# The opening of a two-layer diffusion backbone: modulation weights in column pieces, sums of squares on TensorE

## The chip, the cores and the metric

The kernel runs on one NeuronCore of a Trainium2 chip. The core has TensorE (matrix products, written PE in the trace, its weight loads PEld), VectorE (DVE), ScalarE (ACT), GpSimd (POOL) and SyncE (SP, which here only issues DMAs). Each engine works through its own list of instructions in order. The metric is the device time of one execution in microseconds; lower is better.

## The reference, cut to what matters

Two layers run over 256 latent and 256 context tokens of width 1024. Every sub-layer begins with a norm whose scale and shift come from a conditioning vector, one vector for latent tokens and one for context tokens (two "classes"). The change concerns only the first sub-layer of layer 0:

```python
m_lat = split(silu(c) @ w_ada[l] + b_ada[l], 9)       # shift, scale, gate of three sub-layers
m_ctx = split(silu(c_ctx) @ w_ada[l] + b_ada[l], 9)
y = x * rsqrt(mean(x * x, -1) + EPS)                  # rmsnorm, then * norm_g
h = y * norm_g * (1 + scale) + shift                  # modulate
a, b = split(h @ ffn_w1, 2)                           # D = 1024 -> 2 * 2816
x = x + 0.5 * gate * ((silu(a) * b) @ ffn_w2)
```

Shift and scale of this first norm are the first 2 x 1024 columns of `w_ada[0]`. All nine vectors of the other norms are computed later, beside dense products, by another routine.

## The kernel before, in words

Activations lie transposed: channels on the 128 partitions in 8 chunks (`kc`), 512 tokens along the free side, context in columns 0 to 255, latents in 256 to 511. A dense product is done as three products in a rounded 32-bit format (`three`, lines 230 to 234): weights and activations are each split into a high part (`hi`, a cast on ScalarE, line 219) and a low part (`lo`, a subtraction on VectorE, line 220), and hi x lo, hi x hi and lo x hi are added up in PSUM. The first of the three uses the low part of the activations, so a chunk's products start only when the low parts of both classes are there.

A unit of `ffn_w1` is 128 output columns: 128 x 1024 numbers in one DMA of 512 KB into a ring of four `raw` buffers. Two units, a and b, give one tile of the hidden layer. TensorE's order is the order of the program; the other engines' lists are ordered by a scheduler at build time, by priorities, so an instruction can stand ahead of one that was written earlier.

The opening of the program is `cold_start` (line 413). What stands around the change:

- SyncE issues, in order: the conditioning vector, `x` in 8 DMAs of 256 KB, four DMAs of the first half of the scale's columns (512 columns; `room`, line 164), two units of `ffn_w1`, four DMAs of the first half of the shift's columns, four more units, then the second halves of scale and shift (eight DMAs).
- The sum of squares of each token is a chain over the 8 chunks and two classes: a square on ScalarE (line 257), an addition on VectorE (line 258). Four transpositions on TensorE, a reduction on VectorE, a scaling and a power of -1/2 on GpSimd (lines 263 to 271) give 1/rms per token, and two pairs of transpositions spread it over partitions (line 281; ScalarE copies it to `junk`, line 428).
- Scale and shift are products of `sc` (silu of the two conditioning vectors, padded to 32 columns) with `w_ada` (line 169): four column groups of TensorE at once, each one block of 128 columns, all 8 chunks accumulated. ScalarE copies the result (`rows`, line 174), one transposition brings channels onto partitions (line 177), VectorE adds the bias (line 182) and forms norm_g * (1 + scale) (line 184).
- `norm_part` (line 286) makes one chunk and class of the activations: `u` on VectorE (line 289), the high part on ScalarE (line 291), the low part on VectorE (line 292).
- Six units (`FIRST`) are worked in two parts. Part 0 runs chunks 0 to 3 of units 0-1, 2-3, 4-5; part 1 runs chunks 4 to 7 of units 4-5, 0-1, 2-3. The products for the second halves of scale and shift are fed between the dense products of part 0 and the start of part 1, at the counts listed in `COLD`. After that the program goes on with the other 38 units of `ffn_w1`, one pair at a time.

Of the kernel before, what the change touches and what calls it, by code (L numbers as in the profile page):

```python
# [16 lines left out]
P = 128  # L17
# [33 lines left out]
EARLY = 2  # L51
COLD = ((4, 6, 8, 10, 12, 13), (10, 12, 14, 16, 17, 18))
# [59 lines left out]
def tile_backbone(ctx: ExitStack, tc: tile.TileContext, I, out: bass.AP):  # L112
# [45 lines left out]
    def ada_first(l, mod, part, room):  # L158

        pa = psum()  # L160
        c0 = mod * D + part * 512
        for k2 in range(KC // 2):
            raw = room[:, k2, :]
            nc.sync.dma_start(out=raw.rearrange("p (k c) -> p k c", k=2),
                              in_=I["w_ada0"][k2 * 256:(k2 + 1) * 256, c0:c0 + 512].rearrange("(k p) c -> p k c", k=2))
            for k in range(2):
                kc = 2 * k2 + k
                for j in range(4):
                    mm(pa[32 * j:32 * j + 32, 0:P], sc[:, kc, :], raw[:, k * 512 + j * P:k * 512 + (j + 1) * P],
                       start=kc == 0, stop=kc == KC - 1)  # L170
            yield
        rows = np_.tile([P, 256], F32, tag="rows", name="rows", bufs=1)[:, 0:P]
# [5 lines left out]
        ks = slice(4 * part, 4 * part + 4)  # L178
        v = pt[:, 0:P].rearrange("p (j c) -> p j c", j=4)
        with tc.high_priority(offset=AHEAD):  # L180
            for cls in range(2):
                nc.vector.tensor_tensor(modT[l][:, mod, cls, ks], v[:, :, cls], b_ada[:, l, mod, ks], ALU.add)
                if mod % 3 == 1:
                    nc.vector.scalar_tensor_tensor(amod[l][:, mod // 3, cls, ks], modT[l][:, mod, cls, ks], 1.0,
                                                   norm_g[:, l, mod // 3, ks], ALU.add, ALU.mult)
# [36 lines left out]
    def weights(src, n=1024, extra=None, soon=False, room=None, behind=None):  # L222
        raw = wp.tile([P, 1024], F32, tag="raw", name="raw", bufs=4)
        nc.sync.dma_start(out=raw[:, :n], in_=src)
        hi, lo = room or ((extra or wp).tile([P, 1024], F32R, tag=tag, name=tag) for tag in ("whi", "wlo"))
        with tc.high_priority(offset=AHEAD if soon else WSOON):
            split(hi[:, :n], lo[:, :n], raw[:, :n], behind)
        return hi, lo
# [57 lines left out]
    def norm_part(l, which, h, kc, cls, rb):  # L286
        cs = SLICES[cls]
        u = np_.tile([P, 256], F32, tag="u", name="u", bufs=UB)
        nc.vector.scalar_tensor_tensor(u, x[:, kc, cs], amod[l][:, which, cls, kc:kc + 1], rb, ALU.mult, ALU.mult)
        shift = modT[l][:, 3 * which, cls, kc:kc + 1]  # L290
        lead[cls, kc] = nc.scalar.activation(h[0][:, kc, cs], u, AF.Identity, bias=shift).ins
        nc.vector.scalar_tensor_tensor(h[1][:, kc, cs], u, shift, h[0][:, kc, cs].bitcast(F32),  # L292
                                       ALU.add, ALU.subtract)
# [67 lines left out]
    def ada_all(vectors, pool, junk):  # L361
        if not vectors:
            return
        scb = pool.tile([P, 2, 512], F32, name="scb")
# [12 lines left out]
    def ffn(l, i, classes, out_classes_next, before, vectors):  # L377
# [35 lines left out]
        def cold_start(n):  # L413

            rooms = glo.before(F32, [P, KC, 1024])
            scale, shift = ([ada_first(l, 3 * which + what, part, rooms[:, 4 * (1 - what):4 * (1 - what) + 4, :])
                             for part in (0, 1)] for what in (1, 0))
            for dt in range(KC):
                for at in SLICES:
                    square_sum(dt, at)  # L420
            rows = [rstd_rows(at) for at in SLICES]
            next(scale[0])
            for r in rows:
                next(r)
            rb = junk.rearrange("p (a t) -> p a t", a=2)
            for cls, r in enumerate(rows):
                next(scale[0])
                nc.scalar.copy(rb[:, cls], next(r)[:, 0:256])
            ws = []

            def load(ks):
                for k in ks:
                    ws.append(w1_unit(k, room=kept(k) if k < 4 else None, soon=k < 2))

            for _ in scale[0]:
                pass
            load(range(EARLY))
            for _ in shift[0]:
                pass
            load(range(EARLY, n))  # L440
            pts = [psum() for _ in range(n)]
            beside.at(scale[1], COLD[0])
            beside.at(shift[1], COLD[1])
            for part, order in enumerate(((0, 2, 4), (4, 0, 2))):
                if part:
                    beside.drain()
                with tc.high_priority(offset=AHEAD):
                    for kc in range(4 * part, 4 * part + 4):
                        for cls in (0, 1):
                            norm_part(l, which, h, kc, cls, rb[:, cls])  # L450
                for k in order:
                    for kc in range(4 * part, 4 * part + 4):
# [4 lines left out]
                    if part:  # L457
                        act(k // 2, pts[k], pts[k + 1])
# [926 lines left out]
```

## Time and profile before

| | |
|---|---|
| time, median of 3 runs | 2267.32 us (2265.69 to 2268.48) |
| the profiled execution's own time | 2266.51 us |
| its span, first to last instruction | 2264.7 us |
| first dense product starts | 26.89 us |
| first product behind the six opening units | 67.63 us |
| TensorE busy over the span | 2234.9 us, 99% |

The span is what the trace's rows add up to; 1.8 us of the profiled execution lie outside it. TensorE is nearly always busy, so the time is its list of products plus the stretches in which it waits or runs at the lower of its two clocks, 1.2 in place of 2.4 GHz ("granted clock" 0.50 in the rows). A product's duration in the trace includes its latency; how fast products follow each other is read from the difference of their starts.

### The profile page before, as it was taken

Reading aid. Unit: us, or ns where it says so; the run is one execution under the profiler, and the core shown is the slowest. Engines: PE = TensorE matmul, PEld = TensorE weight load, DVE = VectorE, ACT = ScalarE, POOL = GpSimd, SP = SyncE. Lnnn points to the kernel's source line nnn. Section 1 sums busy time; section 2 is a strip of 40 time slices with the busy share of each in tenths; the row PEclk is TensorE's granted clock in tenths of the full one; section 3 lists DMA queues with packets and bytes.
Section 4 is the critical chain, followed back from the end, with each engine's and each line's share of the span. In section 5 each row is a group of like instructions: output and inputs, shape, how many; then the busy total and the mean of one; then the engine's idle time right before and its main releaser. Section 6 shows DMA issues by size and latency. Waiting matters only on the chain.

```text
span 2264.7 us, 33530 instructions
## 1 busy us (share of the span) xinstructions
PE 2234.9 (99%) x12799; PEld 1935.7 (85%) x12799; DVE 1579.1 (70%) x3388; ACT 934.4 (41%) x1675; POOL 81.3 (4%) x137
## 2 busy tenths in 40 slices
PE   7999999999999999999999999999999999999998
PEld 4888889888888888888888898888898898899998
DVE  5989843887665664676666579998258885768664
ACT  4323222455654553333222232322234675656443
POOL 0000000001001110000000000000000001200000
PEclk9999999999999999999999999999999999999999
DMA  8556542322223332344544436666333244445564
GB/s 305 184 198 204 192 139 89 112 66 75 75 76 93 91 87 84 99 144 140 159 147 149 141 113 208 208 200 195 101 99 112 67 140 121 135 155 169 188 184 131
DMA packets 94033, 315.53 MB, mean 139 GB/s; under 512 B 12928, under 2 KB 13712, under 8 KB 93872
## 3 DMA queue, kind: packets, MB, share of 16 engines
q1 hardware_dynamic: 89072, 308.07, 42.3%
q0 software_dynamic: 2144, 4.36, 1.4%
q8 instruction: 100, 1.64, 0.3%
q10 hardware_dynamic: 2656, 0.96, 0.2%
q14 instruction: 61, 0.50, 0.1%
HBM read 312.30 MB, written 1.05 MB: 138 GB/s over the span
## 4 chain that ended last, share of the span: by engine, by line
PE 86%; issue 9%; DVE 3%; DMA 1%; ACT 1%; SPq 0%; POOLq 0%; POOL 0%; DVEq 0%; ACTq 0%
PE p L232 25%; PE p L233 24%; PE p L234 24%; PE p L649 2%; PE p L650 2%; PE p L651 2%; PE p L674 1%; PE p L916 1%; PE p L1131 1%; PE p L971 1%; PE p L970 1%; PE p L1041 1%; DMA room<-in_w_ada 1%; PE p L893 1%; DVE wlo L220 1%
## 5 line engine op out<-in xcount | busy, mean ns | idle before, releaser
L219 ACT CAST whi<-raw 128x1024 fp32r<-128x1024 f32 (+1 forms) x430 | 444.7, 1035 | 823.7 <-PE p L233 715.7
L220 DVE TENSOR_TENSOR wlo<-raw,whi 128x1024 fp32r<-128x1024 f32 (+1 forms) x430 | 516.6, 1202 | 268.5 <-ACT whi L219 266.8
L232 PE MATMUL p<-h,whi 128*128 128x512 f32 (+1 forms) x1856 | 695.5, 375 | 0.2 <-DVE h L292 0.2
L234 PE MATMUL p<-h,wlo 128*128 128x512 f32 (+1 forms) x1856 | 681.1, 367 | 0.0
L233 PE MATMUL p<-h,whi 128*128 128x512 f32 (+1 forms) x1856 | 681.1, 367 | 0.0
L232 PEld LDWEIGHTS p<-h,whi 128*128 128x128 f32 x1856 | 348.7, 188 | 58.7 <-issue 2.4
L234 PEld LDWEIGHTS p<-h,wlo 128*128 128x128 f32 x1856 | 348.6, 188 | 58.4
L233 PEld LDWEIGHTS p<-h,whi 128*128 128x128 f32 x1856 | 349.1, 188 | 56.5 <-issue 1.9
L233 PE MATMUL p<-ghi,whi 128*128 128x256 f32 (+1 forms) x836 | 278.0, 333 | 0.0
L234 PE MATMUL p<-ghi,wlo 128*128 128x256 f32 (+1 forms) x836 | 277.8, 332 | 0.0
L197 DVE SCALAR_TENSOR_TENSOR junk<-raw,scb 128x512 f32<-128x512 f32 x256 | 176.2, 688 | 112.7 <-DMA raw<-in_w_adaT 112.2
L232 PE MATMUL p<-glo,whi 128*128 128x256 f32 (+1 forms) x616 | 201.9, 328 | 0.0
L197 DVE SCALAR_TENSOR_TENSOR raw<-raw,scb 128x512 f32<-128x512 f32 x256 | 176.8, 690 | 6.2
L233 PEld LDWEIGHTS p<-ghi,whi 128*128 128x128 f32 x836 | 157.9, 189 | 15.4
L234 PEld LDWEIGHTS p<-ghi,wlo 128*128 128x128 f32 x836 | 157.8, 189 | 15.5
L232 PE MATMUL p<-y,whi 128*128 128x256 f32 (+1 forms) x472 | 136.6, 289 | 0.0
L233 PE MATMUL p<-y,whi 128*128 128x256 f32 (+1 forms) x472 | 136.5, 289 | 0.0
L234 PE MATMUL p<-y,wlo 128*128 128x256 f32 (+1 forms) x472 | 136.2, 289 | 0.0
L232 PEld LDWEIGHTS p<-glo,whi 128*128 128x128 f32 x616 | 116.3, 189 | 10.4
L310 DVE SCALAR_TENSOR_TENSOR x<-p,gmod,x 128x256 f32<-128x256 f32 x80 | 36.5, 480 | 81.8 <-PE p L234 81.7
L232 PEld LDWEIGHTS p<-y,whi 128*128 128x128 f32 x472 | 88.7, 188 | 1.8 <-issue 0.2
L233 PEld LDWEIGHTS p<-y,whi 128*128 128x128 f32 x472 | 88.7, 188 | 1.5
(258 smaller groups left out, 2955.6 us busy)
## 6 DMA issues: line engine op xcount, KB each, us to landing
raw<-in_w SPq DMA_DIRECT2D x208, 512.0 KB, 3.5
raw<-in_w_adaT SPq DMA_DIRECT2D x128, 512.0 KB, 3.7
raw<-in_wf SPq DMA_DIRECT2D x106, 512.0 KB, 3.2
raw<-in_w SPq DMA_DIRECT2D x64, 448.0 KB, 3.5
raw<-in_wv SPq DMA_DIRECT2D x24, 512.0 KB, 3.2
raw<-in_wb SPq DMA_DIRECT2D x24, 512.0 KB, 3.3
room<-in_w_ada SPq DMA_DIRECT2D x16, 512.0 KB, 9.5
raw<-in_wo SPq DMA_DIRECT2D x16, 512.0 KB, 3.2
```

Source lines behind the costliest of these rows:

```text
L197: nc.vector.scalar_tensor_tensor(w if cls else junk, w, 1.0, scb[:, cls, :], ALU.mult, ALU.mult, accum_out=acc[:, kc, i, cls:cls + 1])
L219: nc.scalar.copy(hi, src)
L220: nc.vector.tensor_sub(lo, src, hi.bitcast(F32))
L232: mm(dst, w[0][:, wat], a[1][:, aat[0], aat[1]], start=start, stop=False)
L233: mm(dst, w[0][:, wat], a[0][:, aat[0], aat[1]], start=False, stop=False)
L234: mm(dst, w[1][:, wat], a[0][:, aat[0], aat[1]], start=False, stop=stop)
L310: nc.vector.scalar_tensor_tensor(x[:, dt, cs], pt[:, cs], gmod[l][:, which, cls, dt:dt + 1], x[:, dt, cs], ALU.mult, ALU.add)
L649: mm(pts[t], h[0][:, kc, at], w[1][:, wat], start=kc == 0, stop=False)
L650: mm(pts[t], h[0][:, kc, at], w[0][:, wat], start=False, stop=False)
L651: mm(pts[t], h[1][:, kc, at], w[0][:, wat], start=False, stop=kc == KC - 1)
L674: nc.tensor.transpose(pt[:, k * P:(k + 1) * P], a, ident)
L893: mm(pS[:, rs], k[:, at], q[:, rs], start=True, stop=True)
```

## The change

`w_ada`'s 2 x 1024 columns are no longer loaded in four blocks of 512 columns but in six pieces (`PIECES`): four pieces of one chunk (128 columns of scale and 128 of shift), then two pieces of two chunks. Each piece is two DMAs, one for the scale and one for the shift, that fetch all 1024 rows of those columns at once, so one run of memory is 128 (or 256) numbers long where it was 512. On SyncE the pieces are laid between the units of `ffn_w1`: piece 0, units 0 and 1, piece 1, units 2 and 3, piece 2, units 4 and 5, pieces 3 to 5.

Each piece goes its whole way before the dense products that use it: products with `sc` (16 instructions, `begun`), a copy, two or four transpositions, sums over the four column groups, bias and factor, then `norm_part` for its chunks (`ended`), and the dense products of those chunks (`run(i, units)`). The order of dense products is a list written out by hand. Four column groups now hold partial sums over chunks, so VectorE adds four numbers per channel (`tensor_reduce`).

The sums of squares become products: each chunk of x is squared in one instruction over all 512 tokens, alternately on ScalarE and VectorE, and TensorE multiplies four blocks of 128 tokens as weights with one column of ones, accumulating over chunks. `awake(m)` issues m products of ones with ones, 128 x 128, whose result is not used; it stands at three places with m = 6, 4 and 7. Unit 1's low part is issued behind the first low part of the latents.

```diff
-EARLY = 2
-COLD = ((4, 6, 8, 10, 12, 13), (10, 12, 14, 16, 17, 18))
+PIECES = ((0, 1), (1, 2), (2, 3), (3, 4), (4, 6), (6, 8))
...
+    def ada_load(room, e0, e1):
+        w = (e1 - e0) * P
+        got = []
+        for v in (0, 1):
+            at = (2 * e0 + v * (e1 - e0)) % KC
+            raw = room[:, at:at + e1 - e0, :].rearrange("p s c -> p (s c)").rearrange("p (k c) -> p k c", k=KC)
+            nc.sync.dma_start(out=raw, in_=I["w_ada0"][:, v * D + e0 * P:v * D + e0 * P + w].rearrange(
+                "(k p) c -> p k c", k=KC))
...
+    def ada_first(pool, e0, e1, raws, rows):
+        n = e1 - e0
         pa = psum()
...
+        for v, raw in enumerate(raws):
+            for kc in range(KC):
+                g = 32 * (kc % 4)
+                mm(pa[g:g + 32, v * 256:v * 256 + n * P], sc[:, kc, :], raw[:, kc, :], start=kc < 4, stop=kc >= 4)
         with tc.high_priority(offset=AHEAD):
-            nc.scalar.copy(rows, pa[:, 0:P])
+            nc.scalar.copy(rows.rearrange("p (v c) -> p v c", v=2)[:, :, 0:n * P],
+                           pa.rearrange("p (v c) -> p v c", v=2)[:, :, 0:n * P])
         yield
         pt = psum()
-        nc.tensor.transpose(pt[:, 0:P], rows, ident)
+        for v in (0, 1):
+            for e in range(n):
+                at = slice((2 * v + e) * P, (2 * v + e + 1) * P)
+                nc.tensor.transpose(pt[:, at], rows[:, at], ident)
...
+            for v in (1, 0):
+                nc.vector.tensor_reduce(
+                    out=red[:, v], in_=pt.rearrange("p (v e g c) -> p v e c g", v=2, e=2, g=4)[:, v, 0:n, 0:2, :],
+                    axis=AX.X, op=ALU.add)
+                nc.vector.tensor_tensor(modT[0][:, v, :, ks], red[:, v].rearrange("p e c -> p c e"),
+                                        b_ada[:, 0, v, ks].unsqueeze(1).to_broadcast([P, 2, n]), ALU.add)
+                if v:
+                    nc.vector.scalar_tensor_tensor(amod[0][:, 0, :, ks], modT[0][:, 1, :, ks], 1.0,
+                                                   norm_g[:, 0, 0, ks].unsqueeze(1).to_broadcast([P, 2, n]),
+                                                   ALU.add, ALU.mult)
...
         def cold_start(n):
+            room = glo.before(F32, [P, KC, 1024])
+            raws = [ada_load(room, *PIECES[0])]
+            sqs = pool.tile([P, 2, 512], F32, tag="scb", name="sqs", bufs=1)
+            p1 = psum()
+            for kc in range(KC):
+                sq = sqs[:, kc % 2, :]
+                if kc % 2:
+                    nc.vector.tensor_tensor(sq, x[:, kc, :], x[:, kc, :], ALU.mult)
+                else:
+                    nc.scalar.activation(sq, x[:, kc, :], AF.Square)
+                for t in range(NT):
+                    mm(p1[:, t:t + 1], sq[:, t * P:(t + 1) * P], ones[:, 0:1], start=kc == 0 and t == 0,
+                       stop=kc == KC - 1, skip_group_check=True)
...
+            def awake(m):
+                for _ in range(m):
+                    mm(pts[n - 1][:, 0:P], ones, ones, start=True, stop=True)
...
+            load((0, 1))
+            raws.append(ada_load(room, *PIECES[1]))
+            load((2, 3))
+            raws.append(ada_load(room, *PIECES[2]))
+            load(range(4, n))
+            raws.append(ada_load(room, *PIECES[3]))
...
+            awake(6)
...
+            begun(0)
+            awake(4)
+            ended(0)
+            with tc.issue_after(lead[1, 0, "lo"]):
+                for f in rests:
+                    f()
+            begun(1)
+            awake(7)
+            run(0, 0)
+            ended(1)
+            run(1, 0)
+            run(0, 2)
+            begun(2)
+            run(1, 2)
+            ended(2)
+            run(2, 0, 2)
+            begun(3)
+            run(0, 4)
+            ended(3)
+            run(1, 4)
+            run(2, 4)
+            run(3, 0, 2)
+            beside.at(piece(4), (1, 2))
+            run(3, 4)
+            beside.drain()
+            beside.at(piece(5), (4, 8))
+            run(4, 0, 2, 4)
+            beside.drain()
+            for k in (0, 2, 4):
+                run(5, k)
+                act(k // 2, pts[k], pts[k + 1])
```

`run(i, k)` is the dense products of piece i's chunks with units k and k + 1: six products for a piece of one chunk, twelve for a piece of two. `red`, the sums over column groups, is a small new tile; `sqs` holds the squares and later the copied rows.

Three places show how the lists move. First, TensorE's list from the last products of `w_ada` ahead of the dense products to the second pair of chunks; `ghi` and `whi` are the high parts of units (some units lie in the not yet used tile `ghi`), `p` is a PSUM tile, numbers tell tiles apart. Before:

```order
L169 MATMUL p<-room,sc 32x128 x32
L177 MATMUL p<-c_ident,rows 128x128
L232 MATMUL p<-h,ghi 128x512
L233 MATMUL p<-h,ghi 128x512
L234 MATMUL p<-h,ghi 128x512
L232 MATMUL p<-h,ghi 128x512
L233 MATMUL p<-h,ghi 128x512
L234 MATMUL p<-h,ghi 128x512
```

And in the changed kernel:

```order
L177 MATMUL p_253<-room_114,sc_100 32x128 x16
L459 MATMUL p_167<-ones_89 128x128 x7
L250 MATMUL p_162<-h_107,ghi_111 128x512
L251 MATMUL p_162<-h_107,ghi_111 128x512
L252 MATMUL p_162<-h_107,ghi_111 128x512
L250 MATMUL p_163<-h_107,ghi_111 128x512
L251 MATMUL p_163<-h_107,ghi_111 128x512
L252 MATMUL p_163<-h_107,ghi_111 128x512
L186 MATMUL p_286<-c_ident_87,sqs_117 128x128 x2
L250 MATMUL p_162<-h_107,ghi_111 128x512
```

Before, the scale and shift of four chunks stood ahead of the first dense product; now one chunk's do, with the products of piece 1 and seven products of ones, and the two transpositions of piece 1 stand between chunk 0's six dense products and chunk 1's.

Second, VectorE's list around the same place; L220 before and L234 and L245 after are low parts of units, L182 and L184 before and L191, L194 and L197 after bring scale and shift out of PSUM. Before:

```order
L182 TENSOR_TENSOR modT_94<-p,c_b_ada 128x4 x2
L184 SCALAR_TENSOR_TENSOR amod_96<-modT_94,c_norm_g 128x4 x2
L289 SCALAR_TENSOR_TENSOR u<-x,amod_96,junk 128x256 x3
L220 TENSOR_TENSOR ghi<-raw,ghi 128x1024 x2
L182 TENSOR_TENSOR modT_94<-p,c_b_ada 128x4 x2
L292 SCALAR_TENSOR_TENSOR h<-u,modT_94,h 128x256 x2
```

And in the changed kernel, from unit 1's low part on:

```order
L245 TENSOR_TENSOR ghi_111<-raw_172,ghi_111 128x1024
L234 TENSOR_TENSOR ghi_111<-raw_177,ghi_111 128x1024
L191 TENSOR_REDUCE red_289<-p_286 128x2 x2
L194 TENSOR_TENSOR modT0_94<-red_289,c_b_ada_83 128x2 x2
L234 TENSOR_TENSOR ghi_111<-raw_181,ghi_111 128x1024
L197 SCALAR_TENSOR_TENSOR amod0_96<-modT0_94,c_norm_g_85 128x2
L307 SCALAR_TENSOR_TENSOR u_295<-x_74,amod0_96,junk_112 128x256
L307 SCALAR_TENSOR_TENSOR u_299<-x_74,amod0_96,junk_112 128x256
L310 SCALAR_TENSOR_TENSOR h_107<-u_295,modT0_94,h_107 128x256
L310 SCALAR_TENSOR_TENSOR h_107<-u_299,modT0_94,h_107 128x256
```

Before, three `u` were made as soon as the scale was there, ahead of the shift; now scale and shift of a chunk come together, and for chunk 1 a unit's low part (unit 3's) stands between its bias and its factor.

Third, TensorE's list around piece 4, which holds chunks 4 and 5. Before, the last of the second half's transpositions stood here, inside part 0 of units 4 and 5:

```order
L169 MATMUL p<-room,sc 32x128 x8
L232 MATMUL p<-h,whi 128x512
L233 MATMUL p<-h,whi 128x512
L234 MATMUL p<-h,wlo 128x512
L232 MATMUL p<-h,whi 128x512
L233 MATMUL p<-h,whi 128x512
L234 MATMUL p<-h,wlo 128x512
L177 MATMUL p<-c_ident,rows 128x128
```

And in the changed kernel:

```order
L177 MATMUL p<-room,sc 32x256 x16
L250 MATMUL p<-h,whi 128x512
L251 MATMUL p<-h,whi 128x512
L252 MATMUL p<-h,wlo 128x512
L186 MATMUL p<-c_ident,sqs 128x128 x4
L250 MATMUL p<-h,ghi 128x512
L251 MATMUL p<-h,ghi 128x512
L252 MATMUL p<-h,ghi 128x512
```

Piece 4's products stand three dense products ahead of its transpositions, and the row behind the transpositions is already the first dense product with chunk 4; before, 18 dense products of part 0 followed the last transposition.

## Rows read from the trace of the kernel before

**Rows 1.** Stretches: engines' busy us (instructions), granted clock, DMA share, GB/s.

```profile
26.89:67.63 40.74, 40.74 (x274) 30.64 (x275) 31.06 (x71) 16.40 (x30) 0.00 (x0) 0.96 0.70 233
67.63:2264.70 2197.07, 2182.65 (x12388) 1898.54 (x12386) 1536.04 (x3285) 905.83 (x1619) 77.41 (x125) 1.00 0.43 135
10.00:20.00 10.00, 7.30 (x81) 4.34 (x85) 3.84 (x15) 4.03 (x11) 1.39 (x2) 1.00 1.04 408
```

**Rows 2.** Waits of TensorE from 67.6 us on, the longest in total.

```profile
PE p L265 <- DVE ssq L258: 2.4, 3, 1.1
```

**Rows 3.** Chain of waits in the opening: start us, us, what.

```profile
5.92 7.06 DMA room<-in_w_ada
12.99 10.20 DMA room<-in_w_ada
...
24.76 0.34 PE p L177
...
25.12 0.17 DVE modT L182
...
25.86 0.89 DVE h L292 x2
...
26.89 0.47 PE p L232
```

**Rows 4.** Stretches around the fall of the clock, columns as in rows 1.

```profile
26.00:27.00 1.00, 0.11 (x1) 0.14 (x2) 1.00 (x3) 1.00 (x3) 0.00 (x0) 1.00 1.03 420
...
28.00:31.00 3.00, 3.00 (x8) 2.15 (x7) 3.00 (x7) 3.00 (x5) 0.00 (x0) 0.50 1.02 365
```

**Rows 5.** Timeline of TensorE: start us, us, engine, line, operation, out<-in, shapes, count.

```profile
11.86 1.08 PE L169 MATMUL p<-room,sc 128*32 128x128 f32 x16 [11.86 <-DMA room<-in_w_ada]
12.87 1.12 PE L265 MATMUL p<-c_ident,ssq 128*128 128x128 f32 x4
...
33.29 0.39 PE L234 MATMUL p<-h,ghi 128*128 128x512 f32 x1
33.61 0.65 PE L169 MATMUL p<-room,sc 128*32 128x128 f32 x16
34.18 0.50 PE L232 MATMUL p<-h,ghi 128*128 128x512 f32 x1
...
37.94 1.08 PE L169 MATMUL p<-room,sc 128*32 128x128 f32 x32
...
56.75 0.39 PE L232 MATMUL p<-h,ghi 128*128 128x512 f32 x1
...
67.41 0.39 PE L234 MATMUL p<-h,ghi 128*128 128x512 f32 x1
```

**Rows 6.** DMA queues, whole span: packets, MB, share of 16 engines' span.

```profile
q1 hardware_dynamic: 89072, 308.07, 42.3%
...
q10 hardware_dynamic: 2656, 0.96, 0.2%
```

**Rows 7.** Timeline of ScalarE, its first squares.

```profile
5.06 0.72 ACT L254 ACTIVATE ssq<-x 128x256 f32<-128x256 f32 x2 [2.39 <-DMA x<-in_xT]
```

**Rows 8.** Chain of waits later in layer 0, sixteen transpositions: start us, us.

```profile
551.94 1.75 PE p L674 x16
```

**Rows 9.** Groups by line and shape: count, busy us, mean ns, idle before.

```profile
L220 DVE TENSOR_TENSOR ghi<-raw,ghi 128x1024 fp32r<-128x1024 f32 x8 | 9.6, 1218 | 0.0
L668 POOL TENSOR_TENSOR hss<-hss,half 128x4 f32<-128x4 f32 x6 | 6.0, 1008 | 42.3 <-DVE hss L667 42.3
L1113 ACT COPY nT<-p 128x512 f32<-128x512 f32 x32 | 16.9, 596 | 0.7 <-PE p L674 0.4
```

**Rows 10.** Timeline of VectorE in the opening.

```profile
19.69 0.23 DVE L182 TENSOR_TENSOR modT<-p,c_b_ada 128x4 f32<-128x4 f32 x2 [5.03 <-PE p L177]
...
20.15 1.28 DVE L289 SCALAR_TENSOR_TENSOR u<-x,amod,junk 128x256 f32<-128x256 f32 x3
```

More of the change, by code (lines that the diff above doesn't have):

```diff
@@ L156, in tile_backbone @@
     nc.vector.tensor_scalar_mul(sc[:, :, 0:2], th, 0.5)
-    def ada_first(l, mod, part, room):
-        pa = psum()
[L161 to L172, printed above, removed]
+    def ada_load(room, e0, e1):
[6 more added lines that the diff above has]
+                "(k p) c -> p k c", k=KC))
+            got.append(raw)
+        return got
@@ L220, in split, with weights @@
         nc.vector.tensor_sub(lo, src, hi.bitcast(F32))
-    def weights(src, n=1024, extra=None, soon=False, room=None, behind=None):
+    def weights(src, n=1024, extra=None, soon=False, room=None, behind=None, rest=None):
         raw = wp.tile([P, 1024], F32, tag="raw", name="raw", bufs=4)
@@ L413, in cold_start @@
         def cold_start(n):
[L415 to L424, printed above, removed]
@@ L429, in cold_start @@
+            r = np_.tile([P, 4], F32, tag="r", name="r")
+            with tc.high_priority(offset=AHEAD):
+                nc.vector.tensor_scalar(r, p1[:, 0:NT], 1.0 / D, EPS, ALU.mult, ALU.add)
+                nc.gpsimd.tensor_tensor(r, r, half[:, 0:NT], ALU.pow)
             ws = []
+            pts = [psum() for _ in range(n)]
+            def awake(m):
+                for _ in range(m):
+                    mm(pts[n - 1][:, 0:P], ones, ones, start=True, stop=True)
             def load(ks):
@@ L432, in load @@
                 for k in ks:
[L433 to L446, printed above, removed]
+                    ws.append(w1_unit(k, room=kept(k) if k < 4 else None, soon=k < 1, rest=rests if k == 1 else None))
@@ L447, in cold_start, with ended, run @@
+            def ended(i):
+                next(going[i], None)
                 with tc.high_priority(offset=AHEAD):
-                    for kc in range(4 * part, 4 * part + 4):
+                    for kc in range(*PIECES[i]):
                         for cls in (0, 1):
                             norm_part(l, which, h, kc, cls, rb[:, cls])
-                for k in order:
-                    for kc in range(4 * part, 4 * part + 4):
+            def run(i, *ks):
+                for k in ks:
+                    for kc in range(*PIECES[i]):
@@ L456, in cold_start, with piece @@
                             tick()
-                    if part:
-                        act(k // 2, pts[k], pts[k + 1])
+            def piece(i):
+                begun(i)
+                yield
+                ended(i)
+                yield
+            awake(6)
+            p2 = psum()
+            for t in range(NT):
+                nc.tensor.transpose(p2[:, t * P:(t + 1) * P], r[:, t:t + 1].to_broadcast([P, P]), ident)
+            with tc.high_priority(offset=AHEAD):
+                nc.scalar.copy(junk, p2)
+            begun(0)
[29 more added lines that the diff above has]
+                act(k // 2, pts[k], pts[k + 1])
         def warm_start():
```

33 lines of the change are left out of this document (18 added, 15 removed).

## The prediction

> **What bounds the kernel now.** I read the table of stretches first. Behind the opening, from 67.63 us to the end, TensorE is busy 2182.7 of 2197.1 us, and inside the opening from the first dense product it is busy for all of 40.74 us [rows 1]. What little it waits later hangs on its own earlier products: the largest item, the sums of squares of later norms, is 2.4 us in three waits [rows 2]. So nothing later can take up a shift, and the time moves by what happens to one instant: the end of the six opening units, 67.63 us, behind which TensorE's list is the same in both kernels. The chain of waits then shows what sets the start of that stretch: two long DMA pieces (7.06 and 10.20 us, to 23.19), then a transposition at 24.76, VectorE's bias at 25.12, two low parts (0.89 us) and the first dense product at 26.89 [rows 3]. Last the clock: TensorE did almost nothing from 26 to 27, and from 28 to 31 its clock is granted at 0.50, that is 1.2 GHz [rows 4].
>
> **What the 40.7 us before consist of.** Six units are 144 dense products. Undisturbed, 48 of them take 67.63 - 56.75 = 10.88 us, 0.2267 each [rows 5], so 144 take 32.6. A group of 16 products of `w_ada` between two dense ones costs 34.18 - 33.29 - 0.23 = 0.66 us [rows 5]; eight such groups 5.3, two transpositions 0.2. The stretch at half clock is 3.4 us long and loses half of it, 1.7. The sum is 39.8; the 0.9 us left are small gaps, which I also give to the new kernel.
>
> **The start after the change.** Before, 7.52 MB (constants, x, half the scale, two units, half the shift) had landed at 23.19. The new kernel's first dense product stands behind the products of piece 1, ahead of which only 5.42 MB lie: 2.10 MB less, at 408 GB/s [rows 1] 5.1 us earlier, 18.0. But a run of memory in pieces 0 to 3 is 512 bytes, where it was 2 KB. The queue with small packets moves 2656 packets of 361 bytes mean in 0.2% of 16 engines' 2264.7 us, 27 ns each or 213 GB/s over 16 engines; the main queue's packets of 3459 bytes take 172 ns, 322 GB/s with other traffic beside [rows 6]. Bounds for 512 bytes are thus 213 and 408; I take 300, near the middle, which adds 1.9 us for two pieces: 19.9.
>
> The Trainium skill speaks for the upper bound: "DMA: Bandwidth & Descriptors", section Specifications, gives 512 bytes as the least transfer at line rate. By that rule piece 1 lands at 18.0 and the sum falls by 1 to 2 us; by the small-packet row it rises by up to 3. No row here shows 512-byte runs in bulk.
>
> The other way to the start is the norm. x lands from 5.06 on [rows 7], a chunk about every 0.7 us (0.26 MB, at 408 GB/s 0.64 [rows 1]). Each chunk needs 4 products in two passes, 8 weight loads of 128 columns with one moving column. The nearest rows are transpositions, 128 columns of weights and 128 moving: 1.75 / 16 = 0.11 us each at full clock [rows 8], 1.12 / 4 = 0.28 with latency at half clock [rows 5]; one moving column could cost nearly nothing, so 0 to 0.28. Before, the products in the opening ran at half clock: 16 took 1.08 us at 11.86 and 0.65 at 33.61 [rows 5]. At half clock with the weight load as half of a transposition, 64 x 0.13 from 5.8 on ends at 14.1; at full clock x's landing and 0.11 end at 12.5; at 0.28 it is 23.7. Behind it come VectorE's scaling, GpSimd's power (1.0 us [rows 9]), six products of ones, four transpositions, 32 products of piece 0, two copies, four products of ones, two transpositions, and VectorE's chain with the low part of unit 0 (1.22 [rows 9]) in it: 9 us more at full clock to the first low parts, 13.4 at half. Products of ones cost nothing where they lie in such waits; the last seven stand ahead of the first dense product and cost 14 x 0.11 = 1.5 behind piece 1's products (1.1, the 32 of 1.08 [rows 5]). So the first dense product comes at 19.9 + 2.6 = 22.5 at full clock and near 28.8 at half. I take 24.5: 2.4 us earlier than before.
>
> **The dense stretch after the change.** 144 products, 32.6. Products of `w_ada` inside it: pieces 2 and 3 at 1.1 each; pieces 4 and 5 have 256 columns, between 1.1 (instructions decide) and 2.2 (columns decide), I take 1.7: 5.6 in all. Fourteen transpositions at 0.1: 1.4.
>
> New are waits. TensorE works in order, and behind the transpositions of a piece the next row is often a dense product that needs that piece. From the start of the transpositions VectorE begins 0.36 us later (24.76 to 25.12 [rows 3]); two reductions and two additions, small ones at 0.23 a pair, and the factor, 0.12, make 0.6 [rows 10]; two `u` at 0.43 (1.28 / 3 [rows 10]), two low parts 0.88, and 0.15 to the product (25.86 + 0.89 to 26.89 [rows 3]): 2.85 us.
> - Wait A, piece 1: only the two transpositions (0.2) cover it, and unit 3's low part (1.22) stands inside VectorE's chain: 2.85 + 1.22 - 0.2 = 3.9. VectorE also has the low parts of units 1 and 2 in front, and is done with them just in time.
> - Wait B, piece 2: `run(1, 2)` stands ahead of the transpositions, nothing behind: 2.85 - 0.2 = 2.6.
> - Piece 3 is covered by twelve dense products, 2.7.
> - Wait C, piece 4: four transpositions, and three `u` in front of the low parts: 3.5 - 0.4 = 3.1; its second chunk comes 0.5 late. Its transpositions wait 0.1 for the copy of twice 256 numbers (0.60 [rows 9]).
> - Piece 5: twelve products cover all but 0.3, the second chunk is 0.5 late.
> Together 11.0 us, all of them on TensorE's path, since it has nothing else in its list.
>
> **Clock.** Before, one near-idle stretch was followed by one stretch at half clock [rows 4]. Waits A, B and C are three such places; I count two stretches at 3.4 us that cost 1.7 each, between none and three.
>
> The Trainium skill, "TensorE: Matmul & The Clock Gate", section "HAM oscillation — how this bites in real kernels", says that bursts of products between waits fall back to the low clock again and again. By it all three waits are followed by such a stretch, 1.7 us more than I count; with the products of ones doing their work everywhere it is 3.4 less.
>
> **The rest costs nothing, if its cover holds.** The two conditioning vectors for the later `ada` routine reuse the tile of the squares, so their DMA moves from 34 us to behind piece 5's last transpositions, near 62, and that routine's work on VectorE starts some 20 us later; VectorE is busy 1536 of the following 2197 us [rows 1], which leaves room, and TensorE reaches unit 6 only at 79. Without that cover each low part would be late by one step, up to 2 us once. On SyncE, unit 5's DMA waits for unit 1's low part (about 26) with piece 3 behind it, which then lands near 33, and TensorE asks for it near 42. Piece 5 waits for piece 3's products; behind it are the next unit and a small constant, whose cast on ScalarE stands ahead of piece 4's copy: 0 to 1.3 us late, in the range.
>
> **Sum.** 24.5 + 32.6 + 5.6 + 1.4 + 11.0 + 0.9 + 3.4 = 79.4 against 67.6: 11.8 us later. The profiled execution took 2266.51 us (a span of 2264.7 and 1.8 around it), 0.8 below the median of the runs; 2267.3 + 11.8 = 2279. This case's own range is 2272 (start 21.2 of which wait A takes part back, no stretch at half clock, pieces 4 and 5 at 1.1) to 2288 (start 28.8, three stretches, pieces at 2.2, the late copy).
>
> **Rivals.**
> 1. The sums of squares set the start: their 64 weight loads run at half clock at the price of a whole transposition, end at 23.7, and everything behind follows 9 to 10 us later, 33 in place of 24.5. For it: the half clock in the opening before [rows 5]. Against: one moving column, not 128. With the other terms: 2287.
> 2. The early start decides and the kernel is faster. Place: the waits behind transpositions 1, 2 and 4; price: mine are 3.9, 2.6 and 3.1. If products of ones keep the clock at 2.4 GHz from the start and piece 1 lands at 18.0, then 21.0 + 32.6 + 5.6 + 1.4 + 0.9 = 61.5 plus the waits. With all waits together at 1 us that is 62.5, 5.1 earlier: 2262. It decides below 1.6 us of waits. For it: the old opening's VectorE kept pace with TensorE. Against: it had `u` ready before the shift came, and the new lists put dependent rows directly behind each other.
> 3. No change: the same early start with half of my waits, 5.5 to 6, ends at 67.3: 2267. Here the pieces do what the words say (a piece ahead) only in part: piece 3's cover would have to hold for the others too.
>
> **Chances.** Forecast 0.62, rival 1 0.15, rival 2 0.12, rival 3 0.11. A change under 0.2% (4.5 us) can't be told from none here. Faster 0.12, same 0.11, slower 0.77. The range that leaves 2 in 10 out is 2264 to 2288: nearly all of rival 2 and half of rival 1 lie outside.
>
> **What the new profile would show.** The first dense product between 22 and 26 us; TensorE idle by 3 to 4 us after the first six dense products, 2 to 3 after `run(1, 2)`, 3 after piece 4's transpositions, released by VectorE's low part (L310); granted clock 0.50 behind one or two of these; the first product of unit 6 near 79 us; the list behind it as long as before, 2197 us. I am wrong if TensorE waits less than 6 us in all between the first dense product and unit 6, if the products of the squares end after 18 us, or if the part behind unit 6 changes by more than 2 us.

## The result and the profile after

The changed kernel takes 2284.21 us (median of 4 runs, 2282.94 to 2284.77) against 2267.7 us beside it: a ratio of 1.0076, 95% interval 1.0064 to 1.0089. It is slower, as forecast, by 16.5 us where 11.8 were forecast (2279). The time lies in the range, 2264 to 2288.

The profiled execution took 2284.51 us, with a span of 2282.7. First the stretches of the changed kernel, columns as in [rows 1]: the norm before the first dense product, the six opening units, two stretches inside them, and everything behind.

```profile
10.00:20.00 10.00, 10.00 (x47) 10.00 (x48) 1.63 (x4) 1.26 (x2) 0.05 (x1) 1.00 1.09 366
30.06:86.85 56.79, 47.06 (x286) 33.87 (x287) 28.75 (x78) 16.76 (x30) 0.00 (x0) 0.91 0.50 169
34.00:41.00 7.00, 5.12 (x12) 3.80 (x12) 4.01 (x6) 2.79 (x4) 0.00 (x0) 0.51 1.08 355
47.70:51.20 3.50, 3.50 (x10) 2.28 (x9) 0.00 (x0) 0.00 (x0) 0.00 (x0) 0.51 0.00 0
86.85:2282.70 2195.85, 2181.63 (x12388) 1897.69 (x12386) 1543.14 (x3299) 907.67 (x1622) 77.61 (x125) 1.00 0.43 136
```

Behind unit 6's first product TensorE has the same 12388 instructions as before, and 2195.85 us for them where it was 2197.07 [rows 1]. So all of the loss is in the opening: that product comes at 86.85 in place of 67.63, 19.2 us later. The opening units took 40.74 us, without an idle moment; they take 56.79, of which TensorE is busy 47.06. In two stretches its granted clock is 0.51, nearly all of it at 1.2 GHz.

The timeline of TensorE in the changed kernel, columns as in [rows 5]; in brackets the idle time ahead of a row and what ended it:

```profile
5.81 13.78 PE L446 MATMUL p<-ones,sqs 128*128 128x1 f32 x64 [5.81 <-ACT sqs L444]
19.45 2.91 PE L459 MATMUL p<-ones 128*128 128x128 f32 x12
...
26.78 1.83 PE L459 MATMUL p<-ones 128*128 128x128 f32 x14
30.06 0.50 PE L250 MATMUL p<-h,ghi 128*128 128x512 f32 x1 [1.46 <-DVE h L310]
...
31.57 0.38 PE L186 MATMUL p<-c_ident,sqs 128*128 128x128 f32 x2
35.88 0.80 PE L250 MATMUL p<-h,ghi 128*128 128x512 f32 x1 [3.93 <-DVE h L310]
36.47 0.63 PE L251 MATMUL p<-h,ghi 128*128 128x512 f32 x1
36.90 0.63 PE L252 MATMUL p<-h,ghi 128*128 128x512 f32 x1
...
46.66 0.50 PE L250 MATMUL p<-h,ghi 128*128 128x512 f32 x1 [2.63 <-DVE h L310]
...
60.36 1.93 PE L177 MATMUL p<-room,sc 128*32 128x256 f32 x32
...
66.48 0.50 PE L250 MATMUL p<-h,ghi 128*128 128x512 f32 x1 [2.77 <-DVE h L310]
66.82 0.40 PE L251 MATMUL p<-h,ghi 128*128 128x512 f32 x1
67.05 0.40 PE L252 MATMUL p<-h,ghi 128*128 128x512 f32 x1
```

To be seen here: the sums of squares hold TensorE from 5.81 to 19.6, 0.213 us for each of 64 products with a single moving column. The first dense product, which came at 26.89 [rows 3], comes at 30.06. Then TensorE waits three times for VectorE's low part (L310): 3.93, 2.63 and 2.77 us. Behind the first of these waits dense products start 0.43 us apart (36.47, 36.90) where 0.23 is the undisturbed distance [rows 5]; behind the third they keep 0.23 (66.82, 67.05).

What VectorE does in the longest of these waits (timeline of VectorE, changed kernel):

```profile
29.93 1.22 DVE L245 TENSOR_TENSOR ghi<-raw,ghi 128x1024 fp32r<-128x1024 f32 x1
31.06 1.22 DVE L234 TENSOR_TENSOR ghi<-raw,ghi 128x1024 fp32r<-128x1024 f32 x1
32.20 0.23 DVE L191 TENSOR_REDUCE red<-p 128x2 f32<-128x8 f32 x2
32.39 0.24 DVE L194 TENSOR_TENSOR modT<-red,c_b_ada 128x2 f32<-128x2 f32 x2
32.54 1.23 DVE L234 TENSOR_TENSOR ghi<-raw,ghi 128x1024 fp32r<-128x1024 f32 x1
33.69 0.16 DVE L197 SCALAR_TENSOR_TENSOR amod<-modT,c_norm_g 128x2 f32<-128x2 f32 x1
33.88 0.88 DVE L307 SCALAR_TENSOR_TENSOR u<-x,amod,junk 128x256 f32<-128x256 f32 x2
34.94 0.89 DVE L310 SCALAR_TENSOR_TENSOR h<-u,modT,h 128x256 fp32r<-128x256 f32 x2 [0.18 <-ACT h L309]
```

Low parts of three units' weights (L245, L234, L234) run back to back with the chain of piece 1, one of them in its middle. TensorE has nothing to do meanwhile, since the next row of its list needs the end of that chain.

### The profile page after: what moved, and what is told of

It is laid out like the page before. It is cut to its first block, busy times and chain, and to the rows that moved or that the text cites. A ratio compares the mean times of both kernels' runs of the same rounds, so it can differ in the third digit from the quotient of the medians.

```text
span 2282.7 us, 33593 instructions
## 1 busy us (share of the span) xinstructions
PE 2251.5 (99%) x12841; PEld 1953.2 (86%) x12841; DVE 1578.6 (69%) x3393; ACT 932.9 (41%) x1664; POOL 81.2 (4%) x136
## 4 chain that ended last, share of the span: by engine, by line
PE 86%; issue 9%; DVE 3%; ACT 1%; DMA 0%; POOLq 0%; POOL 0%; DVEq 0%; SPq 0%; ACTq 0%
PE p L250 24%; PE p L251 24%; PE p L252 24%; PE p L732 2%; PE p L734 2%; PE p L733 2%; PE p L757 1%; PE p L999 1%; PE p L1214 1%; PE p L1054 1%; PE p L1053 1%; PE p L1124 1%; PE p L976 1%; PE p L446 1%; DVE h L310 1%
## 5 line engine op out<-in xcount | busy, mean ns | idle before, releaser
L234 DVE TENSOR_TENSOR wlo<-raw,whi 128x1024 fp32r<-128x1024 f32 (+1 forms) x430 | 516.6, 1202 | 275.1 <-ACT whi L233 273.9
```

The source lines that it names most:

```text
L234: nc.vector.tensor_sub(lo, src, hi.bitcast(F32))
```

## The experiments

The theory at this point: the loss is (a) a late start, because a product with one moving column costs its whole weight load, and (b) the uncovered waits, with (c) the stretches at 1.2 GHz that follow them. The rivals: the part behind the opening, transfers of `w_ada`, or a clock that falls anyway. Ratios are to the kernel before, run beside each; it took 2266.8 to 2267.7 us there, so a difference between two versions from different sets is good to about 1 us. Edits are shown shortened.

**Quarter sums: (a) taken away.** 32 columns of ones become the weights, and the squares move, 128 columns at a time, one quarter of TensorE for each row block:

```
-  mm(p1[:, t:t + 1], sq[:, t * P:(t + 1) * P], ones[:, 0:1], ...)
+  mm(p1[32 * t:32 * t + 32, 0:P], ones[:, 0:32], sq[:, t * P:(t + 1) * P], ...)
+  (then a copy to lines, one transposition, scaling of one column per quarter)
```

> The changed kernel, but the sums of squares are formed with 32 columns of ones as weights and the squares moving, four column groups at once, instead of the squares as 128-column weights and one column of ones moving. Theory (the 64 weight loads at half clock set the start; they end at 19.6 us): the sums follow x's landing, end near 12 us, the first dense product moves from 30.06 us to between 23 and 26 us, bound by piece 1, and the time falls by 4 to 7 us to 2277 to 2280. Rival a (the DMA of the pieces with runs of 512 bytes sets the start): the first dense product stays after 28 us and the time falls by less than 2 us. Rival b (the long row of products was what raised the clock at 23.8 us): the start is earlier but more of the stretch up to unit 6 runs at half clock, and the time falls by less than 4 us.

2277.66 us (2276.74 to 2278.14), 1.0048 [1.0033, 1.0063]: 6.5 us less than the changed kernel. The groups of the sums, of the changed kernel and then of this one (min/median/max ns of one, first and last start):

```profile
L446 PEld LDWEIGHTS p<-ones,sqs x64: 286/333/333, 5.8 to 19.2; 128*128 128x128 f32 x64
```

```profile
L446 PEld LDWEIGHTS p<-sqs,ones x64: 126/139/155, 5.3 to 11.3; 128*32 128x32 f32 x64
```

```profile
11.23 0.65 PE L446 MATMUL p<-sqs,ones 128*32 128x128 f32 x8 [0.21 <-DVE sqs L442]
...
22.69 0.50 PE L250 MATMUL p<-h,ghi 128*128 128x512 f32 x1
...
28.50 0.79 PE L250 MATMUL p<-h,ghi 128*128 128x512 f32 x1 [3.94 <-DVE h L310]
```

As many products, with a quarter of the weights and 128 times the moving columns, end at 11.9 in place of 19.6, eight in 0.65 us or 0.08 each. The first dense product gains 7.4 us, and the wait of 3.94 us stays. (a) holds, and so does its size.

**The sums alone, on the kernel before.** Its squares and sums, and the rows that spread 1/rms behind them, give way to those of the changed kernel:

```
-  square_sum(dt, at) ... rstd_rows(at)
+  mm(p1[:, t:t + 1], sq[:, t * P:(t + 1) * P], ones[:, 0:1], ...)
```

> The kernel before with one part of the change alone: the sums of squares as products with one column of ones, everything else as before. Theory (these products cost 0.21 us each at half clock and stand in TensorE's list ahead of the products of w_ada): they end near 19.6 us, first dense product near 31 to 33 us instead of 26.9, time 4 to 6 us above before: 2272 to 2274. Rival (only the waits behind the transpositions cost time; the old chain of squares and additions was as late, at 13.6 us plus four transpositions, and the DMA of the shift at 23.2 us hides either): within 2 us of before.

2271.84 us, 1.0025 [1.0015, 1.0035]. The first dense product comes at 30.16 (26.89 [rows 3]), more of the products behind it stand 0.43 us apart, and TensorE waits 1.71 us for a transfer of `w_ada` at 36.59. This part of the change costs about 5 us by itself.

**Quarter sums on the kernel before.**

```
-  square_sum(dt, at) ... rstd_rows(at)
+  mm(p1[32 * t:32 * t + 32, 0:P], ones[:, 0:32], sq[:, t * P:(t + 1) * P], ...)
```

> The kernel before with one edit: its sums of squares as products with 32 columns of ones in four quarters (64 products of 32 columns of weights and 128 moving columns), in place of the squares and sums on the other engines. Its opening waits for the last shares of w_ada (PE at 21.98 and 23.23 waits for a transfer), not for the norm. Theory: the norm is no longer looked at before 21 us, so nothing is gained at the first dense product (26.0 to 27.0 us); what may be gained is the half clock, since PE is busy from 5 us: -0 to -1.7 us, 2265.3 to 2267.3 us. Rival (the sums of squares as products are a loss in themselves): 2269 us or more. Rival 2 (they are a gain in themselves, as in the changed kernel): 2263 us or less.

2268.48 us, 1.0004 [0.9995, 1.0013]: no difference. The first dense product comes at 27.86. Its start is set by shares of `w_ada` (TensorE waits 1.97 us for a transfer at 20.42), so an earlier norm buys nothing there; the hoped-for clock didn't come, its first twelve dense products all stand 0.43 us apart.

**Covered pieces: (b) and (c) taken away.** The same products in another order, so that each piece's chain has at least six dense products beside it that don't need it:

```
-  run(0, 0); ended(1); run(1, 0); run(0, 2); begun(2); run(1, 2); ended(2)
-  run(2, 0, 2); begun(3); run(0, 4); ended(3); run(1, 4); run(2, 4); ...
+  run(0, 0); ended(1); run(0, 2); begun(2); run(1, 0); ended(2); run(1, 2); run(0, 4)
+  begun(3); run(2, 0); ended(3); run(2, 2); run(1, 4); begun(4); run(2, 4); ended(4)
+  run(3, 0, 2); begun(5); run(3, 4); run(4, 0); ended(5); run(4, 2, 4)
```

> The changed kernel with another order of the same dense products: behind the transpositions of every piece stand at least two pairs of units' products that need only earlier pieces (piece 1 has one pair), and the products of a piece's w_ada columns stand further ahead. Nothing is added or left out. Theory (the waits of 3.9, 2.6 and 2.8 us behind the transpositions are on TensorE's path and each drags a stretch at half clock behind it): waits B and C fall under 0.5 us, wait A by 1.4, one or both of the two stretches at half clock go, and the time falls by 6 to 9 us to 2275 to 2278. Rival (VectorE's and ScalarE's lists are the bound, so the waits move to other products): less than 2 us.

2270.84 us (2269.63 to 2271.65), 1.0017 [1.0008, 1.0026]: 13.4 us less than the changed kernel, more than expected. Its timeline of TensorE:

```profile
29.34 0.50 PE L250 MATMUL p<-h,ghi 128*128 128x512 f32 x1 [1.46 <-DVE h L310]
...
33.10 0.50 PE L252 MATMUL p<-h,ghi 128*128 128x512 f32 x1 [0.53 <-DVE ghi L234]
...
35.15 0.50 PE L250 MATMUL p<-h,ghi 128*128 128x512 f32 x1 [0.54 <-DVE h L310]
...
72.18 0.39 PE L250 MATMUL p<-h,whi 128*128 128x512 f32 x1
```

The two are all its waits of note behind the first dense product: 1.07 us, where the changed kernel had 9.7 (the three, and two of 0.2). No dense product in the opening stands 0.43 us from the next. Unit 6 starts 42.84 us after the first dense product, where it was 56.79: 13.9 us less, of which 8.6 are waits, 3.9 what the two stretches at 1.2 GHz cost (measured below), and 1.4 small gaps. The expectation had let wait A fall by 1.4 us, and it fell by 3.4; it had no term for the gaps.

**Products of ones taken away.**

```
-  for _ in range(m):
+  for _ in range(0):
```

> The changed kernel without the 17 products of ones with ones. Theory (at half clock the first six take 2.7 us where GpSimd's power needs about 1.5, the last seven lie ahead of a wait of 1.5 us and are free, and they are what raised the clock at 23.8 us): the first dense product starts about 1 us earlier or at the same time, but the clock rises one stretch later, so the time stays within 3 us of the changed kernel's 2284. Rival a (they hold the clock up for the dense products): 3 to 6 us slower, 2287 to 2290. Rival b (they are only work in TensorE's list): 2 to 4 us faster, 2280 to 2282.

2285.88 us, 1.0084 [1.0067, 1.0101], against 1.0076 with them: not to be told apart. The first dense product comes 1.8 us earlier (28.30; 0.5 of it because the sums start earlier in this trace), but its group and the next two start at 1.2 GHz (28.90 and 29.32 are 0.42 apart), and the clock falls behind the third wait too:

```profile
66.20 0.50 PE L250 MATMUL p<-h,ghi 128*128 128x512 f32 x1 [2.76 <-DVE h L310]
...
67.35 0.63 PE L251 MATMUL p<-h,ghi 128*128 128x512 f32 x1
67.78 0.63 PE L252 MATMUL p<-h,ghi 128*128 128x512 f32 x1
```

Unit 6 comes at 87.63, 59.33 us after the first dense product, where it was 56.79. In these traces the products of ones cost 1.3 to 1.8 us ahead of the first dense product and give 2.5 back behind it; the runs show no net gain.

**Products of ones in the waits: (c) apart from (b).** First 27 and 18 of them in the waits of 3.93 and 2.63 us:

```
   ended(1)
+  awake(27)
   ...
   ended(2)
+  awake(18)
```

> The changed kernel with 27 and 18 more products of ones, in its waits of 3.93 us (ahead of the second piece's first dense product) and of 2.63 us (ahead of the third's); they fill the waits at 0.13 us each and do no work that is needed. Theory (the two stretches at 1.2 GHz behind these waits follow from PE standing idle in them, and cost 2.5 and 1.7 us): no row of the opening's dense products behind 30 us stands 0.43 us from the next, and the time is 2284.2 - 4.2 = 2280.0 us (2279.3 to 2281). Rival (the clock falls for another cause, the stretches come anyway): 2284 to 2285 us. Rival 2 (only the longer wait lets the clock fall): 2281.7 us.

2285.07 us, 1.0079 [1.0066, 1.0091]: no gain. Its timeline of TensorE says why:

```profile
31.62 6.19 PE L459 MATMUL p<-ones 128*128 128x128 f32 x54
37.57 0.47 PE L250 MATMUL p<-h,ghi 128*128 128x512 f32 x1
37.88 0.39 PE L251 MATMUL p<-h,ghi 128*128 128x512 f32 x1
38.11 0.40 PE L252 MATMUL p<-h,ghi 128*128 128x512 f32 x1
...
65.37 0.79 PE L250 MATMUL p<-h,ghi 128*128 128x512 f32 x1 [2.76 <-DVE h L310]
65.97 0.63 PE L251 MATMUL p<-h,ghi 128*128 128x512 f32 x1
66.39 0.63 PE L252 MATMUL p<-h,ghi 128*128 128x512 f32 x1
```

Each product of ones is two rows, 0.22 us together: the fillings overran by 1.8 and 1.1 us. The dense products behind them keep 0.23 us (37.88, 38.11), but those behind the third wait now stand 0.42 us apart (65.97, 66.39), which they didn't in the changed kernel. The overrun, 3.0 us together, and about 1 us in this new stretch use up what the two old stretches had cost: unit 6 again starts 56.79 us after the first dense product. So sized anew, and with the third wait filled:

```
   ended(1)
+  awake(16)
   ...
   ended(2)
+  awake(11)
   ...  behind piece 4, into a bank of its own
+  for _ in range(11): mm(pc[:, 0:P], ones, ones, start=True, stop=True)
```

> The changed kernel with products of ones in its three waits, now sized by what the run before showed (each takes two rows, 0.22 us together, so 27 and 18 of them took 6.19 and 4.18 us, 1.8 and 1.1 us more than the waits had): 16 in the wait of 3.93 us, 11 in that of 2.63, and 11 in that of 2.77 (behind the fifth piece), where the dense products of the run before stood 0.43 us apart. Theory (the stretches at 1.2 GHz follow from PE standing idle, and cost 2.5 and 1.7 us in the changed kernel): no stretch at 1.2 GHz behind 30 us, the first product of unit 6 at 82.5 to 83 us where it was 86.85, and 2284.2 - 4.2 = 2280.0 us (2279 to 2281). Rival 1 (products of ones can't hold the clock, it falls at another place instead): 2282 to 2286 us, with a stretch at 0.43 us in the opening. Rival 2 (the waits are longer with PE busy, since DVE and ACT are then slower): 2281 to 2284 us, no such stretch.

2280.62 us (2279.7 to 2281.5), 1.0061 [1.0048, 1.0073]. Rows of its timeline of TensorE:

```profile
30.51 3.74 PE L459 MATMUL p<-ones 128*128 128x128 f32 x32
34.59 0.50 PE L250 MATMUL p<-h,ghi 128*128 128x512 f32 x1 [0.34 <-DVE h L310]
...
40.26 2.62 PE L459 MATMUL p<-ones 128*128 128x128 f32 x22
43.05 0.50 PE L250 MATMUL p<-h,ghi 128*128 128x512 f32 x1 [0.18 <-DVE h L310]
...
61.33 0.50 PE L250 MATMUL p<-h,ghi 128*128 128x512 f32 x1 [0.31 <-DVE h L310]
...
81.66 0.39 PE L250 MATMUL p<-h,whi 128*128 128x512 f32 x1
```

The waits are as long as before, filled with products that nobody needs, and no stretch at 1.2 GHz is left: unit 6 starts 52.88 us after the first dense product (28.78), 3.9 less than in the changed kernel. Twelve dense products take 2.94 us behind the first wait and 2.97 behind the second, where they took 5.26 and 4.53: the two stretches had cost 2.3 and 1.6 us. (c) is shown, about 4 us of the loss.

**Products of ones on the kernel before,** 14 of them in its wait ahead of the first dense product:

```
+  for _ in range(14): mm(pts[n - 1][:, 0:P], ones, ones, start=True, stop=True)
   beside.at(scale[1], COLD[0])
```

> The kernel before with 14 products of ones in its wait ahead of the first dense product (24.9 to 26.9 us), and nothing else: one part of the change alone. Theory (the dense products of 28.0 to 31.4 us stand 0.43 us apart because PE was idle there; eight or nine of them lose 0.2 us each): 1.4 to 1.7 us less, 2265.3 to 2265.8 us. Rival (the clock falls whether or not PE is busy there, or fourteen products are too few): 2266.5 to 2267.5 us.

2267.66 us, 1.0004 [0.9995, 1.0013]: no difference, for the same error. Its 28 rows of ones took 5.17 us and put the first dense product at 30.45; the dense products behind it then stand 0.23 us apart, and unit 6 follows 39.13 us later where it was 40.74 [rows 1]. So the filling gives 1.6 us of clock back, and the late start takes them away. A filling of the right size wasn't run on the kernel before, so whether a net gain is left there stays open.

**Both mends together.** The covered order with the quarter sums:

> The changed kernel with both mends: each piece behind two groups of six to twelve dense products that don't need it, and the sums of squares as one weight load of 32 columns of ones and 128 moving columns per row block (four quarters of PE). Theory (the cost is the start plus the uncovered waits plus the half clock that follows them, and these add): the first dense product comes at 22.7 us, as with the quarter sums alone (it was 29.3 with the covered list alone), unit 6 begins at 65.0 to 66.5, and the time is 2270.8 - 6.5 = 2264.3 us (2263 to 2266), below the kernel before by 1 to 4 us. Rival 1 (with an earlier start the weights and the later pieces of w_ada, which come over the same DMA engines, are late next): only 2 to 4 us of the 6.5 are left, 2267 to 2269 us, and waits for a transfer show in the opening. Rival 2 (the price lies behind the opening): over 2269 us.

2263.81 us (2263.04 to 2265.33, 11 runs), 0.9987 [0.9978, 0.9996]. The gains add (6.5 and 13.4 alone, 20.4 together), and this version lies below both kernels: 20.4 us below the changed one, and 3.2 below the one before, little but outside the interval. Its first dense product starts at 22.49 and unit 6 at 65.35, 2.3 us ahead of [rows 1]:

```profile
22.49 0.50 PE L250 MATMUL p<-h,ghi 128*128 128x512 f32 x1 [0.71 <-DVE h L310]
...
65.35 0.39 PE L250 MATMUL p<-h,whi 128*128 128x512 f32 x1
```

**The same with fewer products of ones ahead of the first dense product:**

```
-  awake(6)    ...   awake(4)
+  awake(3)    ...   awake(2)
```

> The version with covered pieces and quarter sums, with 3 and 2 of the products of ones where it had 6 and 4 (two rows each): its 12 rows ran from 12.96 to 15.5 us, and the reciprocal roots that the next transposition needs were there at 14.55; its 8 rows ran from 17.40 to 18.40, and the rows that the next transposition needs were there at 17.96. Theory (overfilled waits, 0.9 and 0.4 us): first dense product at 21.2 to 21.8 us (22.49), 2262.5 to 2263.2 us. Rival 1 (the first piece's later transfers or the weights' low parts set the first dense product now): 2263.5 to 2264.5. Rival 2 (with fewer products of ones the clock falls in the opening): 2265 us or more, with dense products 0.43 us apart.

2264.0 us, 0.9986 [0.9977, 0.9995]: the same time. The first dense product comes at 22.42: the products of piece 0 now run slower (32 in 1.94 us; 1.08 with all the ones), so that piece 0's transpositions start at 18.42, where they started at 18.40. What fewer ones save, TensorE loses again on the products behind them; the dense products stay 0.23 us apart. A low part of weights (L234, 1.22 us) stands inside VectorE's chain to the first low parts in both versions.

## Why the prediction was right, and where its sizes were off

**The mechanism.** Slower, because three waits behind transpositions are uncovered: predicted 3.9, 2.6 and 3.1 us, measured 3.93, 2.63 and 2.77. The covered order, which changes nothing else, takes back 13.4 us; in the traces 8.6 are waits and 3.9 the clock behind them. Their working, VectorE's chain from [rows 3] and [rows 10] with one low part in it, held to 0.4 us.

**The start.** This is the mis-sized term: the first dense product was predicted at 24.5 and came at 30.06, beyond even the 28.8 given for half clock. The failed step is the price of a sum's product, taken as 0.13 us with the weight load as half of a transposition; it is 0.213. The sums ended at 19.6, not 14.1, past the 18 us at which the prediction called itself wrong. From their end to the first dense product it took 10.5 us, inside the 9 to 13.4 reckoned; with 14.1 that gives 24.6, so the whole miss of the start lies in this price. The row of 10 to 20 us above gives the granted clock as 1.00, but the rows of products of ones take 0.24 us each at 19.45 and 0.13 at 26.78, so I take the sums to have run at 1.2 GHz; no run had them at 2.4. Rival 1 had the right place, and too high a price (0.28). Its 2287 lies nearer to the result than 2279 does: the late sums are a second cause beside the waits, not one in place of them.

The row that could have told is a transposition at full clock, 0.109 us [rows 8]: by it the load of 128 columns is the whole price, and twice that at half clock is 0.218. The Trainium skill states this, on the page "TensorE: Matmul & The Clock Gate", section "LDWEIGHTS (loading the stationary operand)": the load takes the columns of the weights over 1.2, in ns, whatever the contraction. For 128 columns that is an estimate of 107 ns. The traces agree with it at full clock (0.109), and the sums took twice as much, 0.213. The prediction didn't weigh that rule.

**The transfer.** Piece 1 was taken to land at 19.9, where the upper bound of the rate gave 18.0. In the changed kernel the sums hide it. With quarter sums it shows: TensorE's weight loads wait for the second half of piece 1, here in the quarter sums alone and then in the version with both mends.

```profile
20.44 0.38 PEld L177 LDWEIGHTS p<-room,sc 128*32 128x32 f32 x16 [1.16 <-DMA room<-in_w_ada]
```

```profile
19.38 0.38 PEld L177 LDWEIGHTS p<-room,sc 128*32 128x32 f32 x16 [0.29 <-DMA room<-in_w_ada]
```

These loads start at 20.44 and 19.38, around 19.9, but not for the reason given. By 18 us the queue of the first of these runs had moved 5.45 MB (that of the second 5.31), about what the upper bound asks for (5.42). Between 18 and 20 us it moved mostly the larger packets of the next units, with the last small ones of piece 1 among them (its traffic from 0 to 18, from 18 to 20, and, for the rate of small packets, from 15 to 16.4 us):

```profile
DMA packets 5774, 5.45 MB, mean 303 GB/s; under 512 B 410, under 2 KB 4443, under 8 KB 5774
DMA packets 284, 0.81 MB, mean 403 GB/s; under 512 B 21, under 2 KB 100, under 8 KB 283
DMA packets 896, 0.48 MB, mean 344 GB/s; under 512 B 12, under 2 KB 888, under 8 KB 896
```

So the piece waits for its last packets, and 19.9 was hit with some luck. Why they come late is open. The rate taken, 300 GB/s, was too low: where nearly all packets are small the queue moved 344. The Trainium skill's page "DMA: Bandwidth & Descriptors" (section Specifications) gives 512 bytes as the least transfer at line rate; here runs of that length moved 344 GB/s where longer ones moved 408 [rows 1].

**Clock.** Two stretches were counted, 3.4 us together; there were two, behind the first and the second wait, and they cost 2.3 and 1.6, 3.9 us. The prediction read the Trainium skill's page "TensorE: Matmul & The Clock Gate", section "HAM oscillation — how this bites in real kernels", as putting one behind all three waits. The Trainium skill tells there of bursts that start at the low clock again after each wait, but its waits are longer than the second and third here. The trace shows none behind the third wait, and other runs show one there; so the count of two was no more than a fair guess.

**Small terms.** `w_ada` products inside the opening, transpositions and gaps were 5.6 + 1.4 + 0.9 = 7.9. Measured is what is left of 56.79 after 32.6 of dense products, 9.7 of waits and 3.9 of clock: 10.6. Of it a group with 256 columns takes 1.93 where 1.7 was taken; the covered order has 9.2 in their place (42.84 less 32.6 and 1.07). The rest isn't taken apart.

**The sum.** Against 79.4 the opening ended at 86.85: the start 5.6 later, the clock 0.5, small terms 2.7, the waits 1.3 less. The part behind gave 1.2 back, inside the 2 us allowed. The profiled execution lay 0.3 above its median where that of before lay 0.8 below, so 5.2 of the 7.45 us show in the median.

**The other rivals** fell: an early start (2262) needs under 1.6 us of waits and needs the sums early; only the version with both mends has these, and it reaches 2263.8. No change (2267) needs half of the waits, and 9.7 of the 11.0 us were there.

## What to carry to other kernels

When a long preparation is cut into pieces "one ahead" of the work, count for each piece the work on the bound engine that stands between the request and the need: a piece whose chain on another engine takes 3 us and that has 0.2 us of cover was late each time here, and two of three paid a second time in clock. A product is priced by its weights as well as by its moving columns: let the constant operand be the narrow weight and the data move. Filling a wait with idle products returned the clock and no more, and what they overran was lost again (3.0 of 3.9 us).

## What the runs showed of the hardware

- A product with 128 columns of weights and one moving column took 0.213 us in a stream of 64, at 1.2 GHz by the rows behind it; with 32 columns of weights and 128 moving columns in four quarters, 0.08.
- The length of a wait alone didn't decide whether the clock falls behind it: behind 2.77 us it stayed at 2.4 GHz in the changed kernel and with the quarter sums, and behind 2.76 us it fell to 1.2 for about 3 us when the two earlier waits had been filled, and also with no products of ones at all. What decides is open.
- In a stretch of nearly only 512-byte runs the queue moved 344 GB/s (15 to 16.4 us, quarter sums); the opening as a whole moved 366 between 10 and 20 us, against 408 before [rows 1].
